# One address remainder for the operands of TensorE, and an up projection in products of 256 columns

## The chip, the cores and the metric

The kernel runs on one core of one Trainium2 chip. The metric is the device time of one execution in microseconds (us): the median of 3 runs before is 1488.55 us (1487.88 to 1491.05). TensorE (PE in the profile) multiplies, VectorE (DVE) and ScalarE (ACT) do the element-wise work, SyncE (SP) issues nearly all DMAs. SBUF is the on-chip memory that the engines read, 128 partitions wide; PSUM holds what TensorE writes, in banks of 512 float32 per partition.

## The reference

One decoder layer on x of 256 rows by 2048 columns, float32. `mod` is the vector `c` through a 2048 by 12288 matrix.

```
h = layer_norm(x) * (1 + sc1) + sh1
proj = h @ w_in                              # 2048 x 9760, cut into the parts below
y_nsa = nsa_attention(q, kv, gates)          # compressed, selected and window branches
y_ml  = mlstm(qk, v, if, o)                  # chunkwise matrix memory
merged = sig(g1)*(y_nsa @ w_br_nsa) + sig(g2)*(y_ml @ w_br_ml)
x = layer_norm(ALPHA*x + g1*(merged @ w_o))
h = layer_norm(x) * (1 + sc2) + sh2
a, g = split(h @ w_up)                       # 2048 x 11264: the up projection
u = silu(causal_dwconv(a, conv_w, conv_b)) * g
x = layer_norm(ALPHA*x + g2*(u @ w_down))    # 5632 x 2048: the down projection
```

## The kernel before, in words

All large products run on TensorE in fp32r, a float32 format that rounds. To keep accuracy each operand is split in two: `hi` is the rounded copy, `lo` is the difference. A product is then three, hi times hi, hi times lo and lo times hi. Activations lie transposed in SBUF with both halves (`hT`, `mgT`, `uTt`, `h2T`: per block of 128 rows of the contraction, 256 columns hi, then 256 columns lo). Weights come from HBM as tiles of 128x1024 in seven buffers `w`; `load_split` (L106) casts a tile to `wh` on ScalarE (L112) and subtracts it to `wl` on VectorE (L113). `wh` and `wl` have four buffers each.

Each matmul has a stationary operand (128 columns, loaded by an LDWEIGHTS that the profile shows as PEld) and a moving one, which streams. The LDWEIGHTS of the next matmul runs beside the streaming of this one. There are three ways to multiply:

- `mm_a` (L130): the activation is stationary, the weights stream, 512 columns (392 or 256 in places): projections `ps_a`, `ps_mg`, `ps_br`, `ps_o`, `ps_d`.
- `mm_b` (L124): the weights are stationary, the activation streams in three products of 256 columns: `ps_b`, the first part of the input projection.
- `mm_c` (L120): weights stationary; `wh` against hi and lo side by side, one product of 512 columns into both halves of a bank, then `wl` against hi, 256 columns. The up projection alone uses it, through `wide` (L577), with one bank for `a` and one for the gate. `narrow` (L594) then adds the two halves of each bank into `ag` (a copy on ScalarE, L596, and an addition on VectorE, L597, for each).

The address of an operand within a partition is chosen by the program: small unused tiles (`padx`, `padh`, `padw`, `padu`) and a start offset within a buffer (`OFF`, 16 elements, 64 bytes) shift them. A buffer of `wh` and `wl` is 1024 + 32 elements long, so that neighbouring buffers differ by 128 bytes mod 256.

Stages, in order: the vector `c` times its matrix on VectorE (L186), LayerNorm, the transposes `ps_nT`; 20 `ps_warm` matmuls (L324), which compute nothing that is used, read `identr` and `maskr`, and stand in TensorE's order before the first `ps_b`; the input projection in four groups of the contraction (3, 4, 5 and 4 blocks of 128 rows), each with 24 column blocks of `ps_b` and six column groups of `ps_a`, the tiles of `c`'s matrix for the next group between its weight tiles; attention and mLSTM with `ps_mg` products as filler; merge (`ps_mg`, `ps_br`), output projection (`ps_o`), two LayerNorms, 22 steps of the up projection, half the down projection (`ps_d`), 22 more, the other half, the last LayerNorm.

The order of the instructions on each engine is set when the program is built, by a scheduler that simulates it; each engine then takes its own in that order and waits where an operand is missing. SyncE too issues in order: a load that waits for a free buffer holds up the loads behind it.

Of the kernel before, what the change touches and what calls it, by code (L numbers as in the profile page):

```python
# [7 lines left out]
F32 = mybir.dt.float32  # L8
# [6 lines left out]
P = 128  # L15
S = 256
# [21 lines left out]
WB = (7, 4, 4)  # L38
NU0, NU1 = 4, 1
WARM = 20  # L40
OFF = 16
PADX, PADH, PADW = 16, 8, 32
MORD = (0, 2, 1, 3)
PTV = 2
YA = 2
# [1 line left out]
AW = 392  # L47
A_MO, A_G, A_IF, A_V, A_MV = 0, 1024, 1048, 1056, 1568

C_ID, C_U, C_MASK, C_CADD, C_C01, C_SEL, C_ONE, C_N = 0, 128, 256, 384, 416, 448, 480, 488  # L50
(R_C, R_BADA, R_CW, R_CB, R_FW, R_FB, R_PE, R_NG, R_N) = (0, 16, 112, 144, 152, 284, 328, 392, 400)


@with_exitstack
def build(ctx: ExitStack, tc: tile.TileContext, d, out, dbg=None):
# [13 lines left out]
    prm = p0.tile([P, R_N], F32, name="prm")  # L69
    nc.sync.dma_start(prm, d["prm"])  # L70
    nc.sync.dma_start(cst, d["cst"])
    pad = p0.tile([P, PADX], F32, name="padx")
    xt = p0.tile([P, 2, D], F32, name="xt", tag="t16")
    for t in range(2):
        for c in (0, 1024):
# [3 lines left out]
    ones = cst[:, C_ONE:C_ONE + 1].to_broadcast([P, P])  # L79
    sel4 = cst[:, C_SEL:C_SEL + 32]  # L80
    qsel = cst[:, C_SEL:C_SEL + 1]
    msk = cst[:, C_MASK:C_MASK + P]

    def mm(o, lhsT, rhs, start, stop):
        nc.tensor.matmul(o, lhsT, rhs, start=start, stop=stop)  # L85
# [20 lines left out]
    def load_split(src, oh=0, ol=0):  # L106
# [3 lines left out]
        wh = wp.tile([P, 1024 + 2 * OFF], F32R, name="wh", tag="wh", bufs=WB[1])[:, oh:oh + 1024]  # L110
        wl = wp.tile([P, 1024 + 2 * OFF], F32R, name="wl", tag="wl", bufs=WB[2])[:, ol:ol + 1024]
        nc.scalar.copy(wh[:, :n], t[:, :n])  # L112
        lows.append(nc.vector.tensor_sub(wl[:, :n], t[:, :n], wh[:, :n]))  # L113
        return wh, wl

    def split_into(t, hi, lo):
        nc.scalar.copy(hi, t)
        nc.vector.tensor_sub(lo, t, hi)

    def mm_c(ps, wh, wl, i, xt, k, start, stop):  # L120
        mm(ps, wh[:, i * P:(i + 1) * P], xt[:, k].rearrange("p a b -> p (a b)"), start, False)
        mm(ps[:, 0:S], wl[:, i * P:(i + 1) * P], xt[:, k, 0, :], False, stop)
# [144 lines left out]

    def big(name, offset=0):

        t = p0.tile([P, 2 * KD * S + OFF], F32R, name=name, tag="hT")[:, offset:offset + 2 * KD * S]  # L270
        return t.rearrange("p (k a b) -> p k a b", k=KD, a=2)

    hT = big("hT")
# [69 lines left out]
    run_all(ada_mod(0, GROUPS[0]))  # L343


    gates0 = pg.tile([P, 32 + 2 * NU0 * 512], F32, name="gates0", tag="gates0")[:, 32:]
    gates0 = gates0.rearrange("p (u t n) -> p u t n", u=NU0, t=2)
    ast = ExitStack()
    pa = ast.enter_context(tc.tile_pool(name="pa", bufs=1))
    identr = pa.tile([P, P], F32R, name="identr")  # L350
    maskr = pa.tile([P, P], F32R, name="maskr")
    nc.vector.tensor_copy(identr, ident)
    nc.vector.tensor_copy(maskr, msk)
    accC = pa.tile([P, 4, S], F32, name="accC", tag="c4")
    KT = pa.tile([P, G, 2, 2, P], F32, name="KT")
# [144 lines left out]
    def stream(src, width, per, off=0):  # L500

        tiles = iter(range(src.shape[0]))
        while True:
            wh, wl = load_split(src[next(tiles)][:, :width * per], off, off)
# [4 lines left out]
    wb, wa, wv = (stream(d[n], w, p, o) for n, w, p, o in (("w_in_b", P, 8, OFF), ("w_in_a", AW, 2, 0),  # L509
                                                           ("w_in_v", 512, 2, 0)))  # L510
    k0 = 0
    for gi, kn in enumerate(GROUPS):
# [67 lines left out]
    def wide(w, i0, kt, xt, rate, nm):  # L580

        r = []
        for b in range(2):
            ps = bank(psm, "ps_" + nm)
            for hf in range(kt):
                wh, wl = load_split(w[i0 + b * kt + hf], 0, OFF)
                for k in range(8):
                    mm_c(ps, wh, wl, k, xt[b], hf * 8 + k, hf == 0 and k == 0,
                         hf == kt - 1 and k == 7)
                tk.tick(rate)  # L590
            r.append(ps)
        return r

    def narrow(dst, pss):  # L594
        for b, ps in enumerate(pss):
            nc.scalar.copy(dst[:, b * S:(b + 1) * S], ps[:, S:])  # L596
            nc.vector.tensor_add(dst[:, b * S:(b + 1) * S], ps[:, :S], dst[:, b * S:(b + 1) * S])  # L597
# [320 lines left out]
    def proj_rows(xT, kn, w, base, grow, first, st, hold, rate, nm, hooks=()):  # L918


        n = 0
        hooks = dict(hooks)
        for c in range(3):
            pss = [bank(psm, "ps_%s%d" % (nm, t)) for t in range(2)]
            for i in range(kn // 2):
                wh, wl = load_split(w[base + n])
                n += 1
                for j in range(2):
                    k = 2 * i + j
                    for t in range(2):  # L930
                        mm_a(pss[t], xT, k, t, wh[:, j * 512:(j + 1) * 512],
                             wl[:, j * 512:(j + 1) * 512], k == 0, k == kn - 1)
                tk.tick(rate)
                if n in hooks:
                    hooks[n]()
            for t in range(2):
                residual(pss[t], t, c * 512, 512, grow, first, st)
        later = []
        for c in range(2):
            c0 = 1536 + 256 * c  # L940
            pss = [bank(psm, "ps_%s%d" % (nm, t)) for t in range(2)]
            for k0 in range(0, kn, 4):
                m = min(4, kn - k0)
                keep = hold(c, k0, m) if hold else None
                if keep:
                    t_ = load(w[base + n])
                    wh, wl = keep
                    v = t_[:, :m * 256].rearrange("p (k n) -> p k n", k=m)
                    split_into(v, wh, wl)
                else:  # L950
                    wh, wl = load_split(w[base + n], OFF, OFF)
                    wh, wl = (x[:, :m * 256].rearrange("p (k n) -> p k n", k=m) for x in (wh, wl))
                n += 1
# [32 lines left out]
    hold1 = big("hold1", OFF)  # L986
    hold0 = pg.tile([P, 32 + KD * 256], F32R, name="hold0", tag="gates0")[:, OFF:OFF + KD * 256]
# [10 lines left out]
    n2 = pg.tile([P, 32 + 2 * D], F32, name="n2", tag="gates0")[:, 32:]  # L998
# [118 lines left out]
    padu = pf.tile([P, OFF], F32, name="padu")  # L1117
    hold2 = pf.tile([P, KH - KD, 2, 256], F32R, name="hold2")
    def up(j):
        ag = t2([P, 512], "ag")  # L1120
        narrow(ag, wide(d["w_up"], j * 4, 2, (h2T, h2T), UR, "up"))
        fw = lambda i: prm[:, R_FW + 3 * j + i:R_FW + 3 * j + i + 1]
        av = t2([P, S], "av")
        nc.scalar.activation(av, ag[:, :S], AF.Identity, bias=prm[:, R_FB + j:R_FB + j + 1], scale=fw(2))
        for i in (1, 0):
            sh = 2 - i
            nc.vector.scalar_tensor_tensor(av[:, sh:], ag[:, :S - sh], fw(i), av[:, sh:],
                                           op0=ALU.mult, op1=ALU.add)
        nc.scalar.activation(av, av, AF.Silu)
        nc.vector.tensor_mul(av, av, ag[:, S:])  # L1130
# [15 lines left out]
    hold3 = big("hold3", OFF)  # L1146

    def hold(c, k, m):
        if c == 0:
# [52 lines left out]
def pack(inputs):  # L1202
# [24 lines left out]
    q[:, R_FW:R_FW + 3 * KF] = f["ffn_conv_w"][0].reshape(3, KF, P).transpose(2, 1, 0).reshape(P, 3 * KF)  # L1227
    q[:, R_FB:R_FB + KF] = f["ffn_conv_b"][0].reshape(KF, P).T
# [61 lines left out]
```

## Time and profile before

| | |
|---|---|
| median of 3 runs | 1488.55 us |
| the profiled execution's own time | 1489.3 us |
| its span in the profile | 1487.2 us |
| granted TensorE clock, mean | 0.982 |
| TensorE busy | 1439.7 us (97%) |
| VectorE busy | 1103.1 us (74%) |
| ScalarE busy | 733.1 us (49%) |
| DMA, mean | 252 GB/s |

The span is what the trace covers; 2.1 us of the execution's time lie around it. A matmul's busy time overlaps that of its neighbours, since the array takes the next before the last has drained: what a product costs in a full stream is the distance from one start to the next, so the time of a stretch without gaps divided by the number of its products. That is how a price is read here. [...]

### The profile page before, as it was taken

How to read it: one execution, taken by the hardware profiler on the slowest of the kernel's cores; microseconds unless marked ns; L12 is line 12 of the kernel's file. 1: busy time of each engine (PE TensorE's matmuls, PEld its weight loads, DVE VectorE, ACT ScalarE, POOL GpSimd, SP SyncE). 2: the span in 40 equal slices, each digit the busy share in tenths (PEclk: the TensorE clock that was granted, in tenths of full speed). 3: DMA queues.
4: the chain of work that ended last, by engine and by line, in shares of the span. 5: the costliest groups of instructions: out<-in, count | busy, mean ns of one | idle time of the engine just before them, and what ended most of it. 6: DMA issues, size and time to landing. Idle time of an engine off the chain costs nothing.

```text
span 1487.2 us, 21477 instructions
## 1 busy us (share of the span) xinstructions
PE 1439.7 (97%) x8062; PEld 1238.4 (83%) x8062; DVE 1103.1 (74%) x1653; ACT 733.1 (49%) x1042; POOL 2.1 (0%) x6
## 2 busy tenths in 40 slices
PE   5999999999999999999699999999999999999997
PEld 5998998877667888888688888888898888888886
DVE  7899887888677887689778878864566666665566
ACT  6644443637664444435465555553345555554341
POOL 0000000000000000000000000000000000000000
PEclk8999999999999999999799999999999999999998
DMA  9999897885767998899168878866566555555661
GB/s 360 365 346 347 312 321 262 319 310 183 272 236 264 321 317 319 323 340 335 46 239 281 281 243 279 282 203 189 191 201 191 193 187 191 191 189 192 188 209 58
DMA packets 103783, 374.63 MB, mean 252 GB/s; under 512 B 11648, under 2 KB 11904, under 8 KB 102912
## 3 DMA queue, kind: packets, MB, share of 16 engines
q1 hardware_dynamic: 103680, 373.27, 72.9%
q8 instruction: 63, 1.03, 0.3%
q14 instruction: 40, 0.33, 0.1%
HBM read 371.13 MB, written 2.10 MB: 251 GB/s over the span
## 4 chain that ended last, share of the span: by engine, by line
PE 90%; DVE 6%; ACT 2%; DMA 2%; issue 1%; SPq 0%; DVEq 0%; ACTq 0%
PE ps_up L85 33%; PE ps_d L85 16%; PE ps_mg L85 11%; PE ps_b L85 8%; PE ps_a L85 7%; PE ps_br L85 6%; PE ps_o L85 5%; DVE w L186 1%; PE ps_y L85 1%; DVE wl L113 1%; DVE xz L976 1%; DVE xz L981 1%; PE ps_hid L85 1%; DMA xt<-in_x_dram 1%; ACT wh L112 1%
## 5 line engine op out<-in xcount | busy, mean ns | idle before, releaser
L113 DVE TENSOR_TENSOR wl<-w,wh 128x1024 fp32r<-128x1024 f32 (+1 forms) x478 | 576.4, 1206 | 313.3 <-ACT wh L112 311.0
L112 ACT CAST wh<-w 128x1024 fp32r<-128x1024 f32 (+1 forms) x478 | 494.5, 1036 | 634.2 <-PE ps_up L85 148.8
L85 PE MATMUL ps_up<-h2T,wh 128*128 128x512 f32 x1408 | 490.7, 393 | 0.0
L85 PE MATMUL ps_up<-h2T,wl 128*128 128x256 f32 x1408 | 394.5, 280 | 0.0
L85 PEld LDWEIGHTS ps_up<-h2T,wh 128*128 128x128 f32 x1408 | 265.0, 188 | 57.6 <-DVE h2T L1104 0.2
L85 PEld LDWEIGHTS ps_up<-h2T,wl 128*128 128x128 f32 x1408 | 266.9, 190 | 0.1
L186 DVE SCALAR_TENSOR_TENSOR w<-w,crow 128x1024 f32<-128x1024 f32 x192 | 233.5, 1218 | 0.0
L85 PE MATMUL ps_d<-wh,uTt 128*128 128x512 f32 (+1 forms) x792 | 210.8, 354 | 0.0
L85 PE MATMUL ps_mg<-wh,hT 128*128 128x512 f32 x512 | 172.9, 409 | 0.0
L85 PEld LDWEIGHTS ps_d<-wh,uTt 128*128 128x128 f32 x792 | 139.4, 188 | 22.4
L85 PE MATMUL ps_d<-wl,uTt 128*128 128x512 f32 (+1 forms) x396 | 140.2, 354 | 0.0
L85 PE MATMUL ps_b<-hT,wh 128*128 128x256 f32 x768 | 133.3, 278 | 0.4 <-ACT wh L112 0.4
L85 PEld LDWEIGHTS ps_b<-hT,wh 128*128 128x128 f32 x768 | 115.6, 188 | 4.9 <-issue 3.7
L85 PEld LDWEIGHTS ps_mg<-wh,hT 128*128 128x128 f32 x512 | 97.2, 190 | 25.4 <-issue 4.4
L85 PE MATMUL ps_a<-wh,hT 128*128 128x392 f32 (+1 forms) x384 | 111.9, 367 | 2.6 <-ACT wh L112 2.6
L85 PE MATMUL ps_b<-hT,wl 128*128 128x256 f32 x384 | 104.7, 278 | 0.7 <-DVE wl L113 0.7
L85 PE MATMUL ps_mg<-wl,hT 128*128 128x512 f32 x256 | 101.2, 395 | 0.0
L85 PEld LDWEIGHTS ps_d<-wl,uTt 128*128 128x128 f32 x396 | 74.3, 188 | 11.2
L85 PEld LDWEIGHTS ps_a<-wh,hT 128*128 128x128 f32 x384 | 72.2, 192 | 11.2 <-ACT wh L112 3.3
L85 PEld LDWEIGHTS ps_b<-hT,wl 128*128 128x128 f32 x384 | 71.4, 188 | 1.7 <-DVE wl L113 1.1
L85 PE MATMUL ps_a<-wl,hT 128*128 128x392 f32 (+1 forms) x192 | 70.2, 366 | 0.8 <-DVE wl L113 0.8
L85 PE MATMUL ps_o<-wh,mgT 128*128 128x512 f32 (+1 forms) x224 | 65.7, 377 | 0.0
(254 smaller groups left out, 1297.3 us busy)
## 6 DMA issues: line engine op xcount, KB each, us to landing
w<-in_w_ada_dram SPq DMA_DIRECT2D x192, 512.0 KB, 5.1
w<-in_w_up_dram SPq DMA_DIRECT2D x176, 512.0 KB, 4.4
w<-in_w_down_dram SPq DMA_DIRECT2D x90, 512.0 KB, 3.8
w<-in_w_mg_dram SPq DMA_DIRECT2D x64, 512.0 KB, 4.7
w<-in_w_in_b_dram SPq DMA_DIRECT2D x48, 512.0 KB, 5.4
w<-in_w_br_dram SPq DMA_DIRECT2D x32, 512.0 KB, 5.6
w<-in_w_o_dram SPq DMA_DIRECT2D x32, 512.0 KB, 4.8
w<-in_w_in_a_dram SPq DMA_DIRECT2D x32, 392.0 KB, 4.5
```

The lines of the kernel that those rows point to most:

```text
L85: nc.tensor.matmul(o, lhsT, rhs, start=start, stop=stop)
L112: nc.scalar.copy(wh[:, :n], t[:, :n])
L113: lows.append(nc.vector.tensor_sub(wl[:, :n], t[:, :n], wh[:, :n]))
L186: ins = nc.vector.scalar_tensor_tensor(t, t, 1.0, crow[:, i * 1024:(i + 1) * 1024], op0=ALU.mult, op1=ALU.mult, accum_out=parts[:, row(m), ...
L976: nc.vector.scalar_tensor_tensor(z, z, mv[:, 0:1], lg[:, c * 512:(c + 1) * 512], op0=ALU.subtract, op1=ALU.mult)
L981: nc.vector.scalar_tensor_tensor(z, z, mv[:, 2:3], lb[:, c * 512:(c + 1) * 512], op0=ALU.mult, op1=ALU.add, accum_out=acc)
```

## The change

It moves addresses and rewrites the up projection.

Addresses. The paddings and offsets are new, `wh` and `wl` buffers are 1024 + 64 elements (their distance is then a multiple of 256 bytes). In the table, remainders of the address mod 256, of the moving operand and of the stationary one that is loaded beside it:

| products | before: moving, stationary | after |
|---|---|---|
| `ps_mg`, `ps_a` of 512 | 32 or 160 by buffer, 160 | 160, 160 |
| `ps_br` | 32 or 160, 160 (`y_mlT`) or 32 (`y_nsaT`) | 160, 160 |
| `ps_o` of 512 | 32 or 160, 160 | 160, 160 |
| `ps_d` of 512 | 32 or 160, 32 | 160, 160 |
| `ps_b` (256) | 160, 96 or 224 | 160, 224 |
| `ps_o`, `ps_d` of 256 | 96 or 224, 160 (`ps_o`) or 32 (`ps_d`) | 96, 160 |
| `ps_up` | 512: 160, 96 or 224; 256: 160, 32 or 160 | 256: 160, 224 |

Up projection. `mm_c`, `wide` and `narrow` go; `up` calls `mm_b`, with `a` in the first half of one bank and the gate in the second. The convolution and the multiplication by the gate read PSUM directly.

Two parts of the first loads become loads of their own: the mask `msk` (128x128, out of `cst`) is loaded behind the first weight tiles, and the convolution's weights `ffn` (128x176, out of `prm`) at the up projection.

```
-OFF = 16
-PADX, PADH, PADW = 16, 8, 32
+OFFB, OFFA, OFFN = 16, 48, 64
+PADH, PADW = 8, 16
...
-        wh = wp.tile([P, 1024 + 2 * OFF], F32R, name="wh", tag="wh", bufs=WB[1])[:, oh:oh + 1024]
-        wl = wp.tile([P, 1024 + 2 * OFF], F32R, name="wl", tag="wl", bufs=WB[2])[:, ol:ol + 1024]
+        wh = wp.tile([P, 1024 + OFFN], F32R, name="wh", tag="wh", bufs=WB[1])[:, off:off + 1024]
+        wl = wp.tile([P, 1024 + OFFN], F32R, name="wl", tag="wl", bufs=WB[2])[:, off:off + 1024]
...
     nc.vector.tensor_copy(identr, ident)
+    msk = t2([P, P], "msk")
+    nc.sync.dma_start(msk, d["msk"])
     nc.vector.tensor_copy(maskr, msk)
...
-                    wh, wl = load_split(w[base + n], OFF, OFF)
+                    wh, wl = load_split(w[base + n], OFFA)
...
+    ffn = pf.tile([P, R_FN], F32, name="ffn")
+    nc.sync.dma_start(ffn, d["ffn"])
+
     def up(j):
-        ag = t2([P, 512], "ag")
-        narrow(ag, wide(d["w_up"], j * 4, 2, (h2T, h2T), UR, "up"))
-        fw = lambda i: prm[:, R_FW + 3 * j + i:R_FW + 3 * j + i + 1]
+
+        ps = bank(psm, "ps_up")
+        for b in range(2):
+            for hf in range(2):
+                wh, wl = load_split(d["w_up"][j * 4 + b * 2 + hf], OFFB)
+                for k in range(8):
+                    mm_b(ps[:, b * S:(b + 1) * S], wh, wl, k, h2T, hf * 8 + k, hf == 0 and k == 0,
+                         hf == 1 and k == 7)
+                tk.tick(UR)
+        a, gate = ps[:, :S], ps[:, S:]
+        fw = lambda i: ffn[:, 3 * j + i:3 * j + i + 1]
```

The order on two engines, in the first 45 us. VectorE before: the cast of the mask (`maskr`) is among its first instructions.

```order
L361 MEMSET projA_219 128x2x4
L170 TENSOR_SCALAR prm_68<-prm_68 128x16 x2
L352 CAST identr_211<-cst_67 128x128
L353 CAST maskr_212<-cst_67 128x128
L278 BN_STATS st_x0_116<-xt_72 128x6 x4
L286 BN_AGGR mv_x0_121<-st_x0_116 128x2
```

VectorE now: the same cast stands behind the third `wl` of `w_in_b` (`wl_366`) and the product of a tile of `c`'s matrix with `crow` (`w_335`).

```order
L112 TENSOR_TENSOR wl_297<-w_294,wh_296 128x1024
L329 TENSOR_TENSOR hT_113<-hm_202,hT_113 128x256
L112 TENSOR_TENSOR wl_331<-w_328,wh_330 128x1024
L181 SCALAR_TENSOR_TENSOR w_300,parts_81<-w_300,crow_84 128x1024
L112 TENSOR_TENSOR wl_366<-w_363,wh_365 128x1024
L181 SCALAR_TENSOR_TENSOR w_335,parts_81<-w_335,crow_84 128x1024
L350 CAST maskr_211<-msk_213 128x128
L112 TENSOR_TENSOR wl_403<-w_400,wh_402 128x1024
```

The cast moved from the first instructions to behind the work of the first weight tiles. SyncE now: the load of `msk` is issued behind the fourth tile of `w_in_b` (`w_400`).

```order
L95 DMA w_294<-in_w_in_b_dram 128x1024
L95 DMA w_300<-in_w_ada_dram 128x1024
L95 DMA w_328<-in_w_in_b_dram 128x1024
L95 DMA w_335<-in_w_ada_dram 128x1024
L95 DMA w_363<-in_w_in_b_dram 128x1024
L95 DMA w_370<-in_w_ada_dram 128x1024
L95 DMA w_400<-in_w_in_b_dram 128x1024
L349 DMA msk_213<-in_msk_dram 128x128
L95 DMA w_407<-in_w_ada_dram 128x1024
```

Before, the mask came with the second load of the program. On TensorE nothing moves there: 16 `ps_c`, 32 `ps_nT`, 20 `ps_warm`, then `ps_b`, as before.

## Rows read from the trace of the kernel before

**Rows 1.** The page: the chain that ended last, shares of the span by line.

```profile
PE ps_up L85 33%; PE ps_d L85 16%; PE ps_mg L85 11%; PE ps_b L85 8%; PE ps_a L85 7%; PE ps_br L85 6%; PE ps_o L85 5%; DVE w L186 1%; PE ps_y L85 1%; DVE wl L113 1%; DVE xz L976 1%; DVE xz L981 1%; PE ps_hid L85 1%; DMA xt<-in_x_dram 1%; ACT wh L112 1%
```

**Rows 2.** The chain in order of time: start us, length us, what.

```profile
30.06 8.15 DMA w<-in_w_in_b_dram
...
126.39 18.95 PE ps_a L85 x82
145.34 41.04 PE ps_b L85 x360
186.38 35.09 PE ps_a L85 x180
...
988.03 121.67 PE ps_d L85 x660
1109.70 244.22 PE ps_up L85 x1408
```

**Rows 3.** Timeline of PE, second half: start us, busy us, product. 1200 us: `ps_up`.

```profile
1199.98 0.28 PE L85 MATMUL ps_up<-h2T,wl 128*128 128x256 f32 x1
...
1200.67 0.28 PE L85 MATMUL ps_up<-h2T,wl 128*128 128x256 f32 x1
```

**Rows 4.** The same, `ps_d` of 256 columns, 64 bytes apart, in two places.

```profile
1085.13 0.28 PE L85 MATMUL ps_d<-wl,uTt 128*128 128x256 f32 x1
...
1085.81 0.28 PE L85 MATMUL ps_d<-wl,uTt 128*128 128x256 f32 x1
...
1447.81 0.28 PE L85 MATMUL ps_d<-wl,uTt 128*128 128x256 f32 x1
...
1448.87 0.28 PE L85 MATMUL ps_d<-wl,uTt 128*128 128x256 f32 x1
```

**Rows 5.** The same, `ps_b`, 64 bytes apart, in two places, each behind `ps_hid` products.

```profile
231.56 0.28 PE L85 MATMUL ps_b<-hT,wl 128*128 128x256 f32 x1
...
231.90 0.28 PE L85 MATMUL ps_b<-hT,wl 128*128 128x256 f32 x1
...
260.37 0.28 PE L85 MATMUL ps_b<-hT,wl 128*128 128x256 f32 x1
...
260.72 0.28 PE L85 MATMUL ps_b<-hT,wl 128*128 128x256 f32 x1
```

**Rows 6.** The same, `ps_d` of 512 columns: remainders equal, then 128 apart.

```profile
1002.61 0.39 PE L85 MATMUL ps_d<-wl,uTt 128*128 128x512 f32 x1
...
1006.69 0.39 PE L85 MATMUL ps_d<-wl,uTt 128*128 128x512 f32 x1
...
1008.07 0.40 PE L85 MATMUL ps_d<-wl,uTt 128*128 128x512 f32 x1
...
1011.57 0.39 PE L85 MATMUL ps_d<-wl,uTt 128*128 128x512 f32 x1
```

**Rows 7.** Windows: stretch, us, busy us (instructions) of PE, PEld, DVE, ACT, POOL, clock, DMA.

```profile
988.03:1079.00 90.97, 90.97 (x396) 74.18 (x396) 46.52 (x45) 35.69 (x38) 0.00 (x0) 1.00 0.59 189
...
704.70:707.40 2.70, 2.70 (x25) 2.70 (x25) 2.70 (x6) 2.33 (x2) 0.00 (x0) 1.00 1.00 396
...
126.40:131.00 4.60, 4.60 (x17) 4.60 (x18) 4.23 (x7) 1.53 (x2) 0.00 (x0) 0.64 1.00 409
```

**Rows 8.** Timeline, the first 42 us: start us, busy us, engine, instruction.

```profile
25.46 4.84 PE L324 MATMUL ps_warm<-maskr,identr 128*128 128x512 f32 x20
...
30.71 0.73 PE L85 MATMUL ps_b<-hT,wh 128*128 128x256 f32 x4 [0.41 <-ACT wh L112]
...
37.26 1.22 DVE L186 SCALAR_TENSOR_TENSOR w<-w,crow 128x1024 f32<-128x1024 f32 x1
```

**Rows 9.** The tile `gb` (4 KB): from its DMA's issue to its landing.

```profile
DMA to landing us min/median/max: 9.2/9.2/9.2
```

**Rows 10.** Groups by shape: busy us, mean ns of one | idle us before.

```profile
L597 DVE TENSOR_TENSOR ag<-ps_up,ag 128x256 f32<-128x256 f32 x88 | 36.7, 418 | 0.0
L596 ACT COPY ag<-ps_up 128x256 f32<-128x256 f32 x88 | 32.0, 363 | 0.0
```

More of the change, by code (lines that the diff above doesn't have):

```diff
@@ L48 @@
 A_MO, A_G, A_IF, A_V, A_MV = 0, 1024, 1048, 1056, 1568
-C_ID, C_U, C_MASK, C_CADD, C_C01, C_SEL, C_ONE, C_N = 0, 128, 256, 384, 416, 448, 480, 488
-(R_C, R_BADA, R_CW, R_CB, R_FW, R_FB, R_PE, R_NG, R_N) = (0, 16, 112, 144, 152, 284, 328, 392, 400)
+C_ID, C_U, C_CADD, C_C01, C_SEL, C_ONE, C_N = 0, 128, 256, 288, 320, 352, 360
+(R_C, R_BADA, R_CW, R_CB, R_PE, R_NG, R_N) = (0, 16, 112, 144, 152, 216, 224)
+R_FB, R_FN = 3 * KF, 4 * KF
 @with_exitstack
@@ L71, in build @@
     nc.sync.dma_start(cst, d["cst"])
-    pad = p0.tile([P, PADX], F32, name="padx")
     xt = p0.tile([P, 2, D], F32, name="xt", tag="t16")
@@ L81, in build @@
     qsel = cst[:, C_SEL:C_SEL + 1]
-    msk = cst[:, C_MASK:C_MASK + P]
     def mm(o, lhsT, rhs, start, stop):
@@ L104, in behind, with load_split @@
             mybir.DependencyClass.NoSync, mybir.DependencyReason.DATA), reason="order")
[L106 removed]
+    def load_split(src, off=0):
         n = src.shape[-1]
         t = load(src)
[L110 to L111 removed]
+        wh = wp.tile([P, 1024 + OFFN], F32R, name="wh", tag="wh", bufs=WB[1])[:, off:off + 1024]
+        wl = wp.tile([P, 1024 + OFFN], F32R, name="wl", tag="wl", bufs=WB[2])[:, off:off + 1024]
         nc.scalar.copy(wh[:, :n], t[:, :n])
@@ L118, in split_into @@
         nc.vector.tensor_sub(lo, t, hi)
-    def mm_c(ps, wh, wl, i, xt, k, start, stop):
-        mm(ps, wh[:, i * P:(i + 1) * P], xt[:, k].rearrange("p a b -> p (a b)"), start, False)
-        mm(ps[:, 0:S], wl[:, i * P:(i + 1) * P], xt[:, k, 0, :], False, stop)
     def mm_b(ps, wh, wl, i, xt, k, start, stop):
@@ L268, in big @@
     def big(name, offset=0):
-        t = p0.tile([P, 2 * KD * S + OFF], F32R, name=name, tag="hT")[:, offset:offset + 2 * KD * S]
+        t = p0.tile([P, 2 * KD * S + OFFN], F32R, name=name, tag="hT")[:, offset:offset + 2 * KD * S]
         return t.rearrange("p (k a b) -> p k a b", k=KD, a=2)
@@ L343, in build @@
     run_all(ada_mod(0, GROUPS[0]))
-    gates0 = pg.tile([P, 32 + 2 * NU0 * 512], F32, name="gates0", tag="gates0")[:, 32:]
+    gates0 = pg.tile([P, OFFN + 2 * NU0 * 512], F32, name="gates0", tag="gates0")[:, OFFN:]
     gates0 = gates0.rearrange("p (u t n) -> p u t n", u=NU0, t=2)
@@ L503, in stream @@
         while True:
-            wh, wl = load_split(src[next(tiles)][:, :width * per], off, off)
+            wh, wl = load_split(src[next(tiles)][:, :width * per], off)
             work()
@@ L507, in stream @@
                 yield wh[:, i * width:(i + 1) * width], wl[:, i * width:(i + 1) * width]
-    wb, wa, wv = (stream(d[n], w, p, o) for n, w, p, o in (("w_in_b", P, 8, OFF), ("w_in_a", AW, 2, 0),
+    wb, wa, wv = (stream(d[n], w, p, o) for n, w, p, o in (("w_in_b", P, 8, OFFB), ("w_in_a", AW, 2, 0),
                                                            ("w_in_v", 512, 2, 0)))
@@ L577, in build @@
     dump("projA", projA)
[L580 to L597, printed above, removed]
     def rows_gen(w, i0, tiles, xT, nm):
@@ L985, in build @@
     padw = p0.tile([P, PADW], F32, name="padw")
-    hold1 = big("hold1", OFF)
-    hold0 = pg.tile([P, 32 + KD * 256], F32R, name="hold0", tag="gates0")[:, OFF:OFF + KD * 256]
+    hold1 = big("hold1", OFFA)
+    hold0 = pg.tile([P, OFFN + KD * 256], F32R, name="hold0", tag="gates0")[:, OFFA:OFFA + KD * 256]
     hold0 = hold0.rearrange("p (k a n) -> p k a n", a=2, n=256)
@@ L997, in build @@
                      ((2, turn_late), (4, load_x), (12, lambda: load_ln(lnr, 0)), (22, tk.drain)))
-    n2 = pg.tile([P, 32 + 2 * D], F32, name="n2", tag="gates0")[:, 32:]
+    n2 = pg.tile([P, OFFN + 2 * D], F32, name="n2", tag="gates0")[:, OFFN:]
     n2 = n2.rearrange("p (t n) -> p t n", t=2)
@@ L1116, in build @@
     lnr2 = pf.tile([P, 2, D], F32, name="lnr2")
-    padu = pf.tile([P, OFF], F32, name="padu")
+    padu = pf.tile([P, OFFA], F32, name="padu")
     hold2 = pf.tile([P, KH - KD, 2, 256], F32R, name="hold2")
+    ffn = pf.tile([P, R_FN], F32, name="ffn")
+    nc.sync.dma_start(ffn, d["ffn"])
     def up(j):
-        ag = t2([P, 512], "ag")
-        narrow(ag, wide(d["w_up"], j * 4, 2, (h2T, h2T), UR, "up"))
-        fw = lambda i: prm[:, R_FW + 3 * j + i:R_FW + 3 * j + i + 1]
+        ps = bank(psm, "ps_up")
[8 more added lines that the diff above has]
+        fw = lambda i: ffn[:, 3 * j + i:3 * j + i + 1]
         av = t2([P, S], "av")
-        nc.scalar.activation(av, ag[:, :S], AF.Identity, bias=prm[:, R_FB + j:R_FB + j + 1], scale=fw(2))
+        nc.scalar.activation(av, a, AF.Identity, bias=ffn[:, R_FB + j:R_FB + j + 1], scale=fw(2))
         for i in (1, 0):
             sh = 2 - i
-            nc.vector.scalar_tensor_tensor(av[:, sh:], ag[:, :S - sh], fw(i), av[:, sh:],
+            nc.vector.scalar_tensor_tensor(av[:, sh:], a[:, :S - sh], fw(i), av[:, sh:],
                                            op0=ALU.mult, op1=ALU.add)
         nc.scalar.activation(av, av, AF.Silu)
-        nc.vector.tensor_mul(av, av, ag[:, S:])
+        nc.vector.tensor_mul(av, av, gate)
         u = uTt[:, j % KH]
@@ L1145, in build @@
     st3 = [p0.tile([P, 8, 6], F32, name="st3_%d" % t, tag="st1_%d" % t) for t in range(2)]
-    hold3 = big("hold3", OFF)
+    hold3 = big("hold3", OFFA)
     def hold(c, k, m):
@@ L1212, in pack @@
     c[:, C_ONE:] = 1.0
-    c[:, C_MASK:C_MASK + P] = np.where(i[None, :] > i[:, None], NEG, 0.0)
+    r["msk"] = np.where(i[None, :] > i[:, None], NEG, 0.0).astype(np.float32)
     n = np.arange(16)
@@ L1226, in pack @@
     q[:, R_CB:R_CB + 8] = f["ml_conv_b"][0].reshape(8, P).T
-    q[:, R_FW:R_FW + 3 * KF] = f["ffn_conv_w"][0].reshape(3, KF, P).transpose(2, 1, 0).reshape(P, 3 * KF)
-    q[:, R_FB:R_FB + KF] = f["ffn_conv_b"][0].reshape(KF, P).T
+    fc = np.zeros((P, R_FN), np.float32)
+    fc[:, :R_FB] = f["ffn_conv_w"][0].reshape(3, KF, P).transpose(2, 1, 0).reshape(P, 3 * KF)
+    fc[:, R_FB:] = f["ffn_conv_b"][0].reshape(KF, P).T
+    r["ffn"] = fc
     q[:, R_PE:R_PE + 64] = f["cmp_pe"][0].transpose(2, 0, 1).reshape(P, 64)
```

## The prediction

> **What bounds the kernel now.** I read the shares of the chain of waits first: TensorE's lines make up nearly all of it, with `ps_up` alone at 33% and every other entry that isn't a product at 1% [rows 1]. The chain in order of time then shows long stretches of products and no wait of another engine in them, from 145.34 us (360 `ps_b` in 41.04 us, then 180 `ps_a` in 35.09) to the up projection (1408 products in 244.22) [rows 2]. So a stage is worth its number of products times their distance, and work on VectorE and ScalarE counts only where TensorE waits for it. Next I read the timeline for the distances, at two places for each kind of product, because the change touches nothing else in the full stream; and last the first 42 us, where an order changes and TensorE isn't yet full.
>
> What the distances show. Three products of 256 with the operands 64 bytes apart take 0.34 us in one place and 0.35 in another: `ps_b` 231.56 to 231.90, but 260.37 to 260.72 [rows 5]; `ps_d` six in 0.68 us (113.3 ns each) at 1085, but nine in 1.06 (117.8) at 1447 [rows 4]. There are two paces, and within a stretch I saw one of them; a stall of TensorE, and not an address, stands ahead of a new draw. At 512 columns the remainders decide: equal, 18 products take 4.08 us (226.7 ns); 128 bytes apart, 15 take 3.50 (233.3) [rows 6].
>
> **Part 1: the up projection.** Now a product of 512 and one of 256 make a pair: 244.22 us / 704 pairs = 346.9 ns [rows 2], and 0.345 in the middle of the stage, two pairs from 1199.98 to 1200.67 [rows 3]. The whole stage has 2 x 704 pairs, 488.4 us. Afterwards it has 4224 products of 256, moving 160 and stationary 224. That is exactly the pair of remainders that part of `ps_b` has now. All of `ps_b` in the gapless stretch averages 41.04 us / 360 = 114.0 ns, both paces included [rows 2]. At that price the stage takes 481.5 us, 6.9 less. All at the quick pace (113.3) it is 478.6, 9.8 less; all at the slow one (117.8) it is 497.6, 9.2 more. I take -7, since the row with 360 products is the widest and has the same operands in the same roles.
>
> Speaking for the quick pace: most `ps_b` of the gapless stretch are near it, as a mean of 114.0 between 113.3 and 117.8 says. Against: the stage is entered only twice, so two draws decide 480 us.
>
> [...]
>
> `narrow` goes with it: 88 copies of 363 ns and 88 additions of 418 [rows 10], 32.0 and 36.7 us on engines that are busy 49% and 74%. TensorE covers them, since it runs without a gap there; worth nothing. Without them the bank is released by the convolution's own reads instead, which come at the same place. If that cover were gone, a step's wait would be under 1 us, 44 times; nothing in the chain speaks for it.
>
> **Part 2: products of 512 columns.** In the code, `ps_mg` has 768, `ps_br` 384, `ps_d` 792, `ps_o` 288 and `ps_a` 192, together 2424, of which about half stand 128 apart. 396 of them in 90.97 us, both kinds mixed, take 229.7 ns each [rows 7]; equal ones take 226.7 [rows 6]. 3.0 ns x 2424 = 7.3 us at most. `ps_a` and some `ps_mg` lie beside attention, where TensorE waits for others, so part of it is no gain. I take -5, between -2 and -7.
>
> **Part 3: the other products of 256.** `ps_d` and `ps_o` get moving 96, stationary 160. `ps_o` has this now at one place: 25 starts in 2.70 us. Each lies 0.28 us in the array, so two belong to the edge of the window: 23 x 117.4 [rows 7], the slow pace. `ps_d` is found at both paces already [rows 4]. 528 products x 4.5 ns is 2.4 either way; I take -1, some of `ps_b` included, which leaves 192 apart.
>
> **Part 4: loads.** `ffn` is issued in SP's slot at the second LayerNorm and needed 8 us later or more by the convolution; 0, with its landing hidden by the products. If it were late, up to 9.2 us, the time in which the small `gb` lands [rows 9], less that lead. The first loads are 152 KB smaller, about -0.3.
>
> The mask is another matter. `ps_warm` reads `maskr`, and stands ahead of every `ps_b` on TensorE. Before, it ran from 25.46 for 4.84 us, and `ps_b` began at 30.71 [rows 8]. Now `msk` is issued behind the fourth `w_in_b` tile. That tile was issued at 30.06 and landed 8.15 us later, at 38.2 [rows 2], and a transfer of 4 KB beside such tiles took 9.2 us [rows 9]; so the mask lands at 38.2 to 39.5. VectorE's order agrees: the cast stands behind the product of `w_335` with `crow`, which ended at 37.26 + 1.22 = 38.5 [rows 8]. So `ps_warm` starts near 38.7, after some 12 us in which TensorE does nothing. [...] `ps_b` starts near 45.5, 15 us later (bounds 12.5 to 19). Queued behind the wait on TensorE is the whole kernel; on VectorE, the cast waits with later `wl` behind it, which nobody needs before `ps_b`.
>
> How much of these 15 us is absorbed? In before, TensorE gets 504 `ps_b` and 252 `ps_a` done from 30.71 to 145.34, and is gapless from there [rows 2, 8]. At 114.0 and 35.09 / 180 = 194.9 ns [rows 2] they need 57.5 + 49.1 = 106.6 of those 114.6 us: 8 us of waits can take up lateness, if the weights go on arriving in the meantime, as the seven buffers let them. +7 remains. Bounds: 12.5 - 8 = +4.5, or 0 to 3 if other gaps in attention absorb more; 19 - 8 = +11, or +15 if the buffers fill up and the loads stop.
>
> **The sum.** -7 -5 -1 -0.3 +7 = -6.3. The profiled execution took 1489.3 us, span 1487.2 and 2.1 around it: 1483.0. The median of the runs before is 0.75 lower, so 1482 in terms of medians, with an own range of 1476 to 1487: up between -9.8 and -5, the 512s between -7 and -2, the wait between +4.5 and +10.
>
> **Rivals.** Differences of 0.2%, 3 us, are what a measurement here can tell from none: 1485.6 to 1491.5 is no change.
>
> A. The forecast above: 0.40.
>
> B. The wait at the start is absorbed (0 to 3 us). For it: TensorE waits in attention too. Against: from 145 on the chain shows none for a long while [rows 2]. About 1476: 0.12.
>
> C. One half of the up projection draws the slow pace: 2112 x (117.8 - 114.0) = 8.0 more, 1490: 0.18. For it: `ps_d` did just that between its halves [rows 4].
>
> D. Both halves at the slow pace, the mechanism that makes the change slower: 1482 + 16 = 1498. It decides as soon as somewhat over half of the 4224 products are slow. For it: `ps_o` with 96 and 160 is slow throughout its window [rows 7], and it is 64 apart as well. Against: `ps_b` with the very same remainders mostly isn't. 0.15.
>
> E. The wait costs its upper bound, +12: 1487: 0.09.
>
> F. Addresses decide nothing, and the paces have another cause: the 512s gain 0, the 256s lie between the paces (115.6: 488.3 us, no change), the wait stays: 1489 + 6 = 1495: 0.06. [...] The rows of 512 columns disagree, 233.3 against 226.7 ns for the same product [rows 6], so the chance stays small.
>
> Faster by over 0.2%: A nearly whole, B, and a little of E: 0.53. Within: most of C and E: 0.24. Slower: D, F and the edge of C: 0.23. The range that leaves out about 2 in 10 reaches from 1474 to 1497.
>
> **What the profile after would show.** Steps of the up projection at 0.340 or 0.353 us per three products, the same through a half; 2 x 704 x 3 products in about 481 us. 512-column products at 227 everywhere, none at 233. `ps_warm` starting at 38 to 39 with a low clock at first, `ps_b` near 45, and the stretch that now begins at 145.34 near 152. I am wrong if the up stage takes over 489 us, if the `ps_warm` shift doesn't show behind 145, or if TensorE waits in the up stage for the convolution's reads of the bank.

## The result, and the profile after

The changed kernel takes 1499.54 us, median of 7 runs (1493.57 to 1503.25); the kernel before, beside it, 1489.17 (1487.88 to 1491.16). The ratio is 1.0061, 95% interval [1.0041, 1.0082]: slower by 0.6%. Forecast were 1482 us and a gain. Two things show before any trace: the median lies 17.5 us over the forecast, and the runs scatter over 10 us, where those before scatter over 3. The second is a weaker sign than it looks: in later batches of 17 to 32 runs the kernel before scatters over 7 to 8 us.

The profiled execution took 1496.1 us, span 1494.1. It is one of the quicker ones, which matters below.

The chain of waits in order of time, kernel after (start us, length us, what), to be laid beside [rows 2]:

```profile
36.24 6.62 PE ps_warm L319 x20
42.86 25.44 PE ps_b L84 x216
...
193.13 35.00 PE ps_a L84 x180
...
750.90 132.38 PE ps_up L84 x1167
884.15 107.41 PE ps_up L84 x912
992.44 120.90 PE ps_d L84 x660
1113.34 248.75 PE ps_up L84 x2112
1362.09 113.12 PE ps_d L84 x594
```

Lateness is read by laying the same piece beside its row of before: the 180 `ps_a` start at 193.13 instead of 186.38, 6.7 us late. The second half of the up projection takes 248.75 us instead of 244.22 [rows 2]; 248.75 / 2112 = 117.8 ns, the slow pace from end to end. In the first half 1167 products run at 132.38 / 1167 = 113.4 ns, and the next 912 at 117.8. So the pace changed once, between two neighbouring pieces. TensorE's timeline at that place shows what stands there:

```profile
882.77 0.39 PE L84 MATMUL ps_up<-h2T,wh 128*128 128x256 f32 x2
883.00 0.28 PE L84 MATMUL ps_up<-h2T,wl 128*128 128x256 f32 x1
883.12 1.03 PE L214 MATMUL ps_adar<-cst,modc 128*128 128x128 f32 x8
883.91 0.48 PE L84 MATMUL ps_up<-h2T,wh 128*128 128x256 f32 x2
884.22 0.28 PE L84 MATMUL ps_up<-h2T,wl 128*128 128x256 f32 x1
```

Eight transposes of another job, and no wait. Each triple of the first part takes 0.34 us, each of the second half 0.35 (timeline, same columns, beside [rows 3]):

```profile
800.04 0.28 PE L84 MATMUL ps_up<-h2T,wl 128*128 128x256 f32 x1
...
801.06 0.28 PE L84 MATMUL ps_up<-h2T,wl 128*128 128x256 f32 x1
```

```profile
1199.98 0.28 PE L84 MATMUL ps_up<-h2T,wl 128*128 128x256 f32 x1
...
1201.04 0.28 PE L84 MATMUL ps_up<-h2T,wl 128*128 128x256 f32 x1
```

Three triples lie between the rows of each: 1.02 us and 1.06.

The products of 512 columns did what was forecast. The window of `ps_d` that lies beside the first of [rows 7] holds as many products in 89.50 us as there in 90.97:

```profile
992.50:1082.00 89.50, 89.50 (x396) 74.09 (x395) 46.80 (x46) 35.92 (x38) 0.00 (x0) 1.00 0.62 192
```

Both windows cut off the first products. From the first start to the last in the timelines the 396 products take 227.0 ns each, instead of 230.4. From the first `ps_br` to the first `ps_o` of 256 columns the timelines hold 233.3 us before and 229.7 after; the two `ps_d` pieces of the chain fall by 0.8 and 1.3. Together 5.7 us.

The mask, in the timeline of the first 43 us (beside [rows 8]):

```profile
34.82 1.22 DVE L181 SCALAR_TENSOR_TENSOR w<-w,crow 128x1024 f32<-128x1024 f32 x1
...
35.97 0.22 DVE L350 CAST maskr<-msk 128x128 fp32r<-128x128 f32 x1
...
36.24 6.62 PE L319 MATMUL ps_warm<-maskr,identr 128*128 128x512 f32 x20 [12.71 <-DVE maskr L350]
```

TensorE stood idle 12.71 us until the cast, and the 20 products then took 6.62 us instead of 4.84. The window over them has a mean granted clock of 0.71. Windows of half a microsecond show 0.50 in each from 36.0 to 40.0 us, 0.96 in the next and 1.00 from 40.5 on:

```profile
36.20:42.80 6.60, 6.56 (x21) 5.28 (x22) 2.37 (x3) 0.45 (x1) 0.00 (x0) 0.71 1.03 410
```

### The profile page after: what moved, and what is told of

Read it like the earlier page. It is cut to its first block, busy times and chain, and to the rows that moved or that the text cites. A ratio compares the mean times of both kernels' runs of the same rounds, so it can differ in the third digit from the quotient of the medians.

```text
span 1494.1 us, 24074 instructions
## 1 busy us (share of the span) xinstructions
PE 1439.8 (96%) x9470; PEld 1304.7 (87%) x9470; DVE 1072.4 (72%) x1565; ACT 710.2 (48%) x954; POOL 2.1 (0%) x6
## 4 chain that ended last, share of the span: by engine, by line
PE 86%; DVE 8%; ACT 2%; DMA 2%; issue 1%; SPq 0%; DVEq 0%; ACTq 0%
PE ps_up L84 33%; PE ps_d L84 16%; PE ps_mg L84 11%; PE ps_b L84 7%; PE ps_br L84 6%; PE ps_o L84 5%; PE ps_a L84 4%; DVE w L181 2%; DVE wl L112 2%; PE ps_y L84 1%; DMA w<-in_w_in_v_dram 1%; DVE xz L954 1%; DVE xz L959 1%; ACT wh L111 1%; DMA w<-in_w_in_b_dram 1%
## 5 line engine op out<-in xcount | busy, mean ns | idle before, releaser
L84 PE MATMUL ps_up<-h2T,wh 128*128 128x256 f32 x2816 | 496.2, 281 | 0.5 <-DVE h2T L1082 0.3
L84 PEld LDWEIGHTS ps_up<-h2T,wh 128*128 128x128 f32 x2816 | 430.1, 188 | 1.0 <-DVE h2T L1082 0.5
```

## The experiments

The theory that the traces suggested: with operands 64 bytes apart a stretch of 256-column products has two paces (113.3 and 117.8 ns), and which one it gets is settled where it is entered. Its chief rivals: a draw without a cause in the program, or the addresses alone. All times are medians; "before" is the kernel before in runs on the same chip, 1488.0 to 1489.9. Three chips were used: one for the early mask, the pause, remainder 0 and the old form at one remainder; one for the float32 product, the late transposes, the old form at 64 bytes and all three together; one for the last two. The changed kernel wasn't run again on them: "under the changed kernel" means under the 1499.54 us above.

**The mask loaded early.** The load moves up in the program:

```
+    msk = t2([P, P], "msk")
+    nc.sync.dma_start(msk, d["msk"])
...
     nc.vector.tensor_copy(identr, ident)
-    msk = t2([P, P], "msk")
-    nc.sync.dma_start(msk, d["msk"])
```

> The changed kernel with the mask's load issued behind the four loads of x, as one small load of its own, so that ps_warm has its operand early again. Theory (the late mask costs what the prediction says): ps_warm starts near 25 us instead of 36.2, the 180 ps_a products that start at 193.1 us start about 7 us earlier, near 186, and the time falls by about 7 us against the changed kernel, to about 1492 in the median (1489 to 1495, the paces of the 256-column products being as variable as before). Rival (the early stage is bound by the arrival of weights, the mask is only a bystander): ps_b starts earlier but waits more, the stretch near 193 moves by less than 2 us, and the time stays at 1499.

Measured: 1489.45 us (12 runs, 1483.74 to 1494.90), ratio to before 1.0008 [0.9994, 1.0022]. The chain of waits has the `ps_a` back at their old place, while the up projection keeps its two paces to the hundredth of a microsecond:

```profile
185.99 35.00 PE ps_a L84 x180
...
743.72 132.38 PE ps_up L84 x1167
876.98 107.41 PE ps_up L84 x912
...
1106.16 248.75 PE ps_up L84 x2112
```

7.1 us earlier at the `ps_a`, 7.2 at the up projection and 7.2 in the profiled times (1488.9 against 1496.1), with the same paces. The late mask cost 7, as forecast. The medians differ by 10; what the other 3 are, these runs don't show.

**A pause ahead of the second half.** ScalarE writes into the bank that the next product fills:

```
         ps = bank(psm, "ps_up")
+        if j == KH:
+            nc.scalar.copy(ps[:, :8], ends[-1][:, :8])
```

> The changed kernel with one short stall of TensorE ahead of the second half of the up projection: ScalarE copies 8 columns of the last ps_d bank into the bank of the next ps_up, so that its first product waits for a round trip (0.5 to 1 us). Order and addresses are the same. Theory (the pace of 256-column products with operands 64 bytes apart is set where a stretch is entered: out of a full stream at 117.8 ns, after a stall mostly at 113.3, and kept until the next stall): the 2112 products of the second half run at 113.3, the stage of 248.75 us takes 239.5, and the time falls by 8 to 9 us against the changed kernel, to about 1491. Rival 1 (the pace is a draw that doesn't depend on how the stretch is entered): slow or quick with the same odds as before, no difference on average, plus 1 us. Rival 2 (the remainders of ps_up alone set it): 117.8 as before, 1500.

Measured: 1491.25 us (12 runs). Ten of them lie between 1487.2 and 1494.2, two at 1499.3 and 1499.5. The profile fell on one of these two, and there the second half ran slow (2112 products in 250.56 us). The window behind the pause, in that trace:

```profile
1114.80:1118.50 3.70, 3.70 (x18) 3.70 (x19) 1.23 (x2) 0.00 (x0) 0.00 (x0) 0.55 0.78 228
```

From the start of the last `ps_d` to that of the first `ps_up` 2.1 us passed instead of 0.5 to 1, since ScalarE's copy stood behind a cast and then waited 0.55 us for VectorE. TensorE sat idle for 1.83 us of them:

```profile
1114.59 0.15 ACT L1105 COPY ps_up<-ps_d 128x8 f32<-128x8 f32 x1 [0.55 <-DVE zt L887]
...
1114.80 0.51 PE L84 MATMUL ps_up<-h2T,wh 128*128 128x256 f32 x2 [1.83 <-ACT ps_up L1105]
```

The mean granted clock of the next 3.70 us is 0.55, near the 0.50 of the windows at `ps_warm`, and 18 products took these 3.70 us, where 18 x 0.118 are 2.1. So this pause was dear: some 2 us of waiting and 1.6 more at that clock. The shorter times of ten runs would fit a quick half, but the trace shows a slow one; by itself this run settled nothing.

**A float32 product ahead of the second half.** No wait in it, and nothing reads its result:

```
         ps = bank(psm, "ps_up")
+        if j == KH:
+            tc.keep_in_program_order(nc.tensor.matmul(ps[:, :S], ident, lnr2[:, 0, :S], start=True, stop=True))
```

> The changed kernel with one float32 product of 256 columns, whose result is overwritten, ahead of the second half of the up projection, in place of the pause of e2_pause (which lasted 2.1 us and brought the granted clock to its low level for 3.5 us). In all traces so far a float32 product of ps_hid stands ahead of the ps_b that run at the quick pace. Theory (the entry sets the pace): the second half, 2112 products, runs at 113.3 ns in most executions, the float32 product costs 0.4 to 0.9 us, the clock stays at its high level, and the time is about 1499.5 - 9.5 + 0.7 = 1491. Rival 1 (only a real wait of TensorE resets the pace): 117.8, about 1500. Rival 2 (a draw without regard to the entry): half of the runs at 1490 and half at 1500.

Measured: 1486.23 us, 13 under the changed kernel. Ten of 12 runs lie between 1484.5 and 1487.5; the profiled one is one of the other two (1494.35). Its chain of waits:

```profile
752.95 137.55 PE ps_up L84 x1167
891.37 107.41 PE ps_up L84 x912
...
1120.97 239.39 PE ps_up L84 x2112
```

The second half is quick: 239.39 us against 248.75, 9.4 less, with the same addresses and order. Here it is the first half that ran slow, 137.55 us for what took 132.38 in the changed kernel's profile; that is 5.2 of the some 8 us between this run and the ten, whose traces weren't kept. The entry itself, in TensorE's timeline:

```profile
1120.14 0.28 PE L84 MATMUL ps_d<-wl,uTt 128*128 128x256 f32 x1
1120.26 0.28 PE L84 MATMUL ps_d<-wh,uTt 128*128 128x256 f32 x1
1120.38 0.59 PE L1104 MATMUL ps_up<-lnr,cst 128*128 128x256 f32 x2
1120.62 0.59 PE L84 MATMUL ps_up<-h2T,wh 128*128 128x256 f32 x2
1121.04 0.28 PE L84 MATMUL ps_up<-h2T,wl 128*128 128x256 f32 x1
```

From the last `ps_d` to the first `wl` product 0.78 us, instead of 3 x 0.118: it costs 0.43 us. Rival 1 (only a wait resets the pace) is out. Of the 13 us in the median this trace accounts for 9; the forecast was 1491, and the other 4 us stay open. Nor does the run tell which property of the inserted product counts, its format, its operands or its being another product at all.

**The transposes behind the first half.** A generator that takes both halves of `g2` and issues the transposes when the ticker is drained:

```
-            for c in range(2):
-                tk.add(ada_rows(5, g2, c))
+            tk.add(ada_rows_late(5, g2))
```

> The changed kernel with the eight transposes (ps_adar) that stand in the middle of the first half of the up projection, near 883 us, moved behind that half. In the traces of the changed kernel, e1_mask_early, e2_pause and e4_up_0_apart the pace after them was the slow one. Theory (they are an entry, and the pace drawn ahead of them would otherwise last): the first half is one stretch of one pace, at 113.3 ns in most executions; 911 products x 4.5 ns = 4.1 us less, so about 1495.5 in the median. Rival (the pace changes by itself, after a while or with the buffers): a change within the half stays, and the time is 1499.

Measured: 1495.44 us, 4.1 under the changed kernel (10 runs, 1490.46 to 1503.82). In its profile the first half is one piece of one pace, the slow one:

```profile
745.54 244.96 PE ps_up L84 x2079
```

244.96 / 2079 = 117.8. The median is the forecast's, but by luck as far as this trace goes: "quick in most executions" it doesn't show. A slow stretch can't tell either whether a quick one would have lasted. The last experiment below can: with the transposes out of the way, 2016 products stayed quick to the end of the half.

**Remainders of the up projection.** Its weights at the same remainder as the activation, in the new form:

```
-                wh, wl = load_split(d["w_up"][j * 4 + b * 2 + hf], OFFB)
+                wh, wl = load_split(d["w_up"][j * 4 + b * 2 + hf], 0)
```

> The changed kernel with the weights of the up projection at remainder 160, the same as the moving operand, instead of 64 bytes on. Theory (the pace is set by the entry, for any distance that allows both): the second half, entered out of the full stream of ps_d, runs at 117.8 or slower, all in all 1498 to 1503. Rival (0 apart has one pace, as 512 columns have): one pace throughout both halves; at 113.3 up takes 479 us and the time is about 1482, at over 117.8 it is 1500 or more.

Measured: 1510.92 us. 253.43 us for the 2112 products, 120.0 ns each, in the first half as well:

```profile
752.71 140.13 PE ps_up L84 x1167
...
1124.90 253.43 PE ps_up L84 x2112
```

One pace, slower than both at 64 bytes, as the rival has it; the theory's 1498 to 1503 is missed by 8 us. So addresses decide which paces there are here, 120.0 ns at 0 apart and 113.3 or 117.8 at 64, and of the two distances that were run in this form, 64 bytes is the better one.

The old form (a product of 512 columns and one of 256, two banks added up), all operands at one remainder:

```
+            for hf in range(2):
+                wh, wl = load_split(d["w_up"][j * 4 + b * 2 + hf], 0)
+                for k in range(8):
+                    mm_c(ps, wh, wl, k, h2T, hf * 8 + k, hf == 0 and k == 0, hf == 1 and k == 7)
...
+            nc.scalar.copy(ag[:, b * S:(b + 1) * S], ps[:, S:])
+            nc.vector.tensor_add(ag[:, b * S:(b + 1) * S], ps[:, :S], ag[:, b * S:(b + 1) * S])
```

> The changed kernel with the up projection of the kernel before (one product of 512 columns and one of 256 per step, two banks added by ScalarE and VectorE), but with moving and stationary operand at the same remainder (160, 160). The late mask and all other addresses stay as changed. Theory (addresses alone give the gain at 512, the late mask costs 7, and the new form of the up projection costs what its slow pace takes): the pair takes 226.7 ns for its 512 columns and 113 to 117 for its 256, 340 to 344 instead of 346.9, up takes 479 to 485 us, and the time is about 1489 + 7 - 5 - 6 = 1485 (1481 to 1490), with less scatter between runs than the changed kernel. Rival (equal remainders gain nothing where the activation streams): pair 346.9 as before, 1490 to 1492.

Measured: 1500.09 us (1498.33 to 1502.95), with the late mask in it. A miss: in the first piece a pair takes 131.52 us / 759 x 2 = 346.6 ns, as before, and in the second half (1115.19 to 1363.92 us) 353.3, slower than before.

```profile
753.61 131.52 PE ps_up L84 x759
...
1115.19 248.73 PE ps_up L84 x1408
```

The same with the early mask and all weights 64 bytes off (`OFFB` for the 0 above):

> The changed kernel with the mask loaded early and the up projection in the old form, 512 and 256 columns, all its weights 64 bytes from the moving operand (in e3_old_up_equal, where they were at the same remainder, a pair took 353.3 ns: 236.5 at 512 and 116.8 at 256). Theory: a pair takes at most the 346.9 ns of the kernel before, and the products of 512 columns elsewhere bring their 5 us: 1482 to 1484, with little scatter. Rival (the 512-column addresses elsewhere bring nothing in the time): 1488. If the products of 256 columns run at 113.3 in it, 343.5 a pair, it is 1478.

Measured: 1492.70 us (1490.17 to 1494.24). 248.74 us for the half, 353.3 a pair again, 235.0 and 118.3: 4% above 226.7 and 113.3 in both. Also a miss.

Then the two apart, `wl` at the same remainder:

```
-                wh, wl = load_split(d["w_up"][j * 4 + b * 2 + hf], OFFB)
+                wh, wl = load_split(d["w_up"][j * 4 + b * 2 + hf], OFFB, 0)
```

> e8_old_up_64 with the two kinds of the old up projection at different distances: wh 64 bytes from the moving operand (512 columns), wl at the same remainder (256 columns). In the kernel before they stood at 64 or 192 and at 128 or 0, changing with the buffer, and a pair took 346.9 ns in every stretch; at 64 and 64 a pair took 353.3 (235.0 and 118.3), at 0 and 0 346.7 in one stretch and 353.3 in another. Theory (products of 512 columns have a slow and a quick pace too, entered as at 256, and mixed distances keep a stretch between them): 346.9 a pair, about 1484 to 1486, with a scatter of 2 to 3 us. Rival 1 (the changing buffers made the middle pace): 353.3 a pair, 1492 as e8_old_up_64. Rival 2 (64 for wh and 0 for wl is quick): 340 a pair, 1476.

Measured: 1484.51 us (12 runs, 1480.33 to 1490.73), ratio to before 0.9973 [0.9958, 0.9989]. The load that runs beside a product is that of the next (in the trace of before the load of a 256's `wl` starts at 1200.10 us with a 512, and its own product at 1200.33): the 512 here stands beside `wl` (0 apart), the 256 beside the next `wh` (64 apart). The chain of waits:

```profile
744.61 129.19 PE ps_up L84 x759
874.68 106.40 PE ps_up L84 x608
...
1102.83 246.40 PE ps_up L84 x1408
```

129.19 us for 759 products is 340.4 a pair, and 350.0 in the other two pieces. Two paces again, with products of 512 columns: rival 2 is right in one piece and nobody in the rest. The time lies in the theory's range by luck, since its 346.9 stands in no piece. The changing remainders of the kernel before gave neither, but 346.9 in every stretch (131.63 us for 759 products, 105.45 for 608, 244.22 for 1408).

**All three together.** Early mask, late transposes, float32 product:

> The changed kernel with all three: the mask loaded early (e1_mask_early), the transposes behind the first half (e6_adar_late), the float32 product ahead of the second half (e5_f32_entry). Theory: the gains add up, 1499.5 - 7 - 4 - 9 = 1479 to 1480, under both kernels; the up projection takes 479 us plus its entries. Rival (the pace is a draw at every entry, with about even odds): 1479 in some executions, up to 1492 in others, median near 1486.

Measured: 1482.06 us (11 runs, 1472.32 to 1486.76), ratio to before 0.9940 [0.9921, 0.9960]. In the profile the first half is slow and the second quick:

```profile
743.78 244.96 PE ps_up L84 x2079
...
1111.81 239.39 PE ps_up L84 x2112
```

So the rival is right of the first half.

**A second float32 product**, ahead of the second step of that half:

```
-        if j == KH:
-            tc.keep_in_program_order(nc.tensor.matmul(ps[:, :S], ident, lnr2[:, 0, :S], start=True, stop=True))
+        if j in (1, KH):
+            tc.keep_in_program_order(nc.tensor.matmul(ps[:, :S], ident, cst[:, :S], start=True, stop=True))
```

> e7_three with a second float32 product of 256 columns, ahead of the second step of the first half of the up projection (in the profile of e7_three this half ran at the slow pace, 2079 products in 244.96 us, and the second half, behind its float32 product, at the quick one, 2112 in 239.39). Theory (a float32 product ahead makes the quick pace likely, more so than the transposes of ps_n): both halves at 113.3 ns in most executions; the runs gather at the low end of those of e7_three (1472.3 to 1486.8), median 1473 to 1477. Rival (the entry of the first half stays an even draw): scatter and median as e7_three, 1482.

Measured: 1475.99 us (6 runs, 1471.09 to 1484.34), ratio to before 0.9909 [0.9886, 0.9932]. This is under both kernels, by 13.9 us and 23.6. Both halves are quick (228.50 / 2016 = 113.3):

```profile
752.48 228.50 PE ps_up L84 x2016
...
1104.06 239.39 PE ps_up L84 x2112
```

That the second product made the first half quick isn't shown. It stands at 751.89 us, and the step ahead of it already ran at 113.3 ns, 48 products in 5.44 us:

```profile
746.33 0.28 PE L84 MATMUL ps_up<-h2T,wl 128*128 128x256 f32 x1
...
751.77 0.28 PE L84 MATMUL ps_up<-h2T,wl 128*128 128x256 f32 x1
```

The runs scatter over 13 us, as those with one product (14), and the two intervals of the ratio overlap. So theory and rival aren't separated here.

**All entries counted.** In the twelve traces, stretches of 256-column products without a gap, at least 18 long, the stationary operand 64 bytes (mod 256) on from the moving one, by what stands ahead of them:

| ahead | quick | slow | other |
|---|---|---|---|
| products of 512 columns without a gap | 0 | 65 | 3, slow and then quick |
| products of 392 columns without a gap | 1 | 5 | 0 |
| float32 product of 256 columns (`ps_hid`, or the ones added) | 96 | 1 | 0 |
| float32 transposes, `ps_adar` in the up projection | 0 | 4 | 0 |
| float32 transposes, `ps_n` ahead of the up projection | 3 | 3 | 0 |
| a stall of TensorE | 16 | 7 | 1, between |

At this distance the entry goes with the pace, nearly always for two kinds of it: behind products of 512 columns 68 stretches of 68 began slow, behind a float32 product 96 of 97 were quick. Not every quick `ps_b` has a float32 product ahead of it, as the expectation of the float32 experiment has it: 15 of the 16 quick stretches behind a stall are `ps_b`. For the second half of the up projection that is shown by experiment: behind `ps_d` alone it was slow in three traces of three, behind the float32 product quick in three of three, and on one chip both ways. For the beginning of the first half no cause is shown. The same instructions led to either pace behind `ps_n`; the three slow cases come from one chip, on which no quick one was profiled, so that the chip has a part in it isn't excluded. The three stretches that changed are `ps_b` near 151 us (pause, float32 product, late transposes); ahead of the change stands one distance of 135 ns, a short stall.

The entry isn't all. In the kernel before the remainders change with the weight tile, and there the pace goes with them in two places. Behind the same `ps_hid` products its `ps_b` runs quick with the weights at 224, 64 bytes on from the activation, and slow with the weights at 96, 192 bytes on; the table leaves out the latter, three stretches and all slow:

```profile
238.38 2.93 PE ps_b L85 x24
241.88 3.02 PE ps_b L85 x24
245.47 2.93 PE ps_b L85 x24
248.97 3.02 PE ps_b L85 x24
```

And its `ps_d` from 1079 us on changes pace five times in one stretch without a gap, each time where the moving operand goes from 96 (192 apart) to 224 (64 apart) or back:

```profile
1079.13 0.28 PE L85 MATMUL ps_d<-wl,uTt 128*128 128x256 f32 x1
...
1084.78 0.28 PE L85 MATMUL ps_d<-wl,uTt 128*128 128x256 f32 x1
...
1090.23 0.28 PE L85 MATMUL ps_d<-wl,uTt 128*128 128x256 f32 x1
...
1094.47 0.28 PE L85 MATMUL ps_d<-wl,uTt 128*128 128x256 f32 x1
```

48 products take 5.65 us, 48 take 5.45 and 36 take 4.24: 117.7, 113.5 and 117.8 ns. But from 1444.9 us on `ps_d` is slow at nearly all of both remainders, and `ps_b` near 160 us is quick at both. So which pace a distance allows, and which one a stretch then gets, aren't settled by one rule. Why a full stream leads to the slow pace and a float32 product to the quick one, these runs don't show.

## Why the prediction was wrong

**The step that failed** is the price of the new products: "At that price the stage takes 481.5 us, 6.9 less [...] I take -7, since the row with 360 products is the widest and has the same operands in the same roles." Measured in the profile: +1.2 us in the first half with its beginning (from its first product to the first `ps_d`, 251.6 us against 250.4) and +4.5 in the second, 5.7 instead of -7. The row of 114.0 ns was a fair price of `ps_b`, but `ps_b` is cut by stalls and by `ps_hid`, and these are entries that mostly led to the quick pace (16 of 24 and 96 of 97 in the count above). The up projection has other entries: its second half follows the slow `ps_d` without a gap, and that follows products of 512 columns. By the count above that entry led to the slow pace each time (68 of 68), so it was no draw. 2112 products at 117.8 instead of 113.3 ns are 9.4 us, and the float32 product won back just these.

The row that said so was quoted: `ps_o` at 96 and 160, slow throughout its window [rows 7], entered out of a full stream. I read it as a matter of its remainders and weighed it against more rows of `ps_b`, where I should have asked what stood ahead of either. I also had one draw for each half; the transposes near 883 make two of the first. A draw "behind a stall" was right as far as it went, but not the only way in. "Within a stretch I saw one of them" and "not an address" were wrong: the quick `ps_d` at 1085 [rows 4] is a piece between two slow ones of the same stretch, and the remainder changes at its ends.

**Rival D** (both halves slow, 1498) is nearest to the measured time, and the median of 1499.5 lies 3.4 us above the profiled execution. With the first 1167 products slow as in the profile of the float32 experiment (137.55 against 132.38), 5.2 us come on top of 1496.1. That most of the seven runs had it so would fit their times, but only the profiled one has a trace.

**The late mask** was right in mechanism: +7 forecast, 6.7 at the `ps_a`, and 7.2 taken back by the early load. That the size fits so well is in part luck, since two terms were each too large by 3 us. `ps_warm` started at 36.2 and not 38.7, since VectorE came to the cast earlier (its product ahead of the cast ended at 34.82 + 1.22 = 36.0, not 38.5). No run shows the 6.8 us that the forecast has from there to `ps_b` (38.7 to 45.5), nor its bounds of 12.5 and 19; what the run showed is 6.62 us for the 20 products at a mean granted clock of 0.71. So `ps_b` began 12.0 us late and not 15 (42.70 instead of 30.71), and 5.3 us of it were absorbed and not 8.

**The 512 columns** were right: 5.7 us measured with `ps_o` and `ps_d` of 256 in it, -5 and -1 forecast. The -1 wasn't: the first 264 `ps_d` of 256 columns went from 115.6 to 117.8 ns, 0.6 us more, and the other 264 and `ps_o` stayed slow.

**`narrow` and the convolution's loads** cost and gained nothing visible: in the second half the products follow each other at 117.8 ns without a wait.

**Rival F** (addresses decide nothing) is out: at 256 columns 0 apart gives 120.0 ns and 64 apart 113.3 or 117.8, and with equal remainders `ps_d` of 512 columns went from 230.4 to 227.0.

**The range** (1474 to 1497) left out the median because it gave the two slow halves together 0.15.

## What to carry to other kernels

A price per instruction, read from a mean, is that of the ways in which its stretches begin (here 114.0 ns in `ps_b`, 117.8 in the second half of the up projection): look at what stands ahead of each, and price a new stretch by the entry that it will have. Look also at whether its operands' addresses change on the way. Where a kernel's runs scatter more than before, two paces are one thing to look for; compare the length of the same piece in several traces rather than medians alone. An operand needed by the first instruction of a full engine belongs among the first loads, however small it is: here one of 64 KB, loaded late, cost 7 us.

## What the runs showed of the hardware

Two paces that last: 113.3 or 117.8 ns for 256 columns with operands 64 bytes apart, kept over more than 2000 products where the remainders stayed the same. Where they changed with the weight tile, the pace could change with them, without a gap (117.7, 113.5, 117.8 ns in `ps_d` before). A single float32 product of 256 columns, at 0.43 us, decided 9.4 us. Products of 512 columns with the activation moving had paces of their own (340.4, 346.6 to 346.9, 350.0, 353.3 ns a pair of 512 and 256), although `ps_d` and `ps_mg`, with the weights moving at equal remainders, showed one, 226.7 ns (96 `ps_mg` in 21.76 us in the changed kernel; 227.0 for the 396 `ps_d` with their beginning). Behind an idle time of 1.83 us the mean granted clock was 0.55 over the next 3.70 us; behind one of 12.71 us it was 0.71 over 6.60 us.
